# Nine seven-product steps instead of eight, with one weight sum done by an accumulating DMA

## The chip, the cores and the metric

The kernel runs on one core of one Trainium2 chip. The metric is the device time of one execution in microseconds (us). Three executions of the kernel before took 1774.49, 1775.84 and 1777.14 us; their median is 1775.84. The profile is of a further execution.

## The reference: what is computed

The input x has 256 rows of 4096 float32 values. One layer is computed: RMS norm, a projection to q, k, v and a gate (4096 x 16384 weights, `w_in`), stick-breaking attention over 32 heads of 128, the gate, a projection back (4096 x 4096, `w_out`), a residual add and a final RMS norm.

```python
def attn_branch(xn, w_in, w_out):
    proj = xn @ w_in
    q, k, v, g = jnp.split(proj, 4, axis=-1)
    ...                                  # 32 heads: o = stick_breaking_attention(q, k, v)
    return (o * jax.nn.silu(g)) @ w_out

def reference(x, norm_attn, w_in_attn, w_out_attn, ...):
    h = x
    for i in range(DEPTH):               # DEPTH is 1: the attention layer alone
        h = h + attn_branch(rms_norm(h, norm_attn), w_in_attn, w_out_attn)
    return rms_norm(h, final_norm)
```

Nearly all arithmetic is the two projections, over 256 rows and 335 MB of float32 weights.

## The kernel before, in words

**Precision.** A float32 operand is held as two fp32r parts, a high one (`wh`, `nh`) and a remainder (`wl`, `nl`). ScalarE (ACT) rounds a weight block to `wh`, VectorE (DVE) subtracts to get `wl`, and a product of two blocks is three matmuls of 128 x 128 by 128 x 512: wh with h, wl with h, wh with l (`mm3`). The row parts are the stationary operand, the weights the moving one.

**Units, steps, products.** The work is 21 units in a row. Units 0 to 15 are the columns of `w_in`, each with 256 columns of q, k, v and gate; units 16 to 20 are the columns of `w_out`. A unit has 16 steps; a step takes 256 of the 4096 rows of the weights, as two 128-row chunks, for two column groups. So a step is a 2 x 2 block product: row blocks A11, A12, A21, A22 (two halves of the 256 rows of x by two chunks) with weight blocks of two loaded tiles, tile 0 and tile 1, each with chunk 0 and chunk 1. Units 0, 1 and 16 are plain: eight products per step, each added to one of four sums. Units 2 to 15, 17 and 18 are mixed: their steps with a number in `SEVEN` (L42) take seven products of Strassen's kind, and the other steps take eight products arranged so that they add to the same seven sums. Units 19 and 20 are single: four products per step. A seven-step needs sums of weight blocks (`sums`, L386) and sums of row blocks (`build`, L493).

**What a step costs the converters.** An eight-step converts each of its two tiles as one block of 128 x 1024 (`piece`, L410: one cast on ACT, one subtraction on DVE). A seven-step converts tile 0, then one 128 x 512 chunk of tile 1, then makes its sums in place of the tiles by four additions of 128 x 512 on DVE, and converts both tiles again. So it has three conversions of 128 x 1024 and one of 128 x 512.

**Buffers.** Weight tiles land in a ring of seven `raw` tiles of 512 KB (two DMAs of 256 KB from the SP queue each), converted blocks in a ring of five pairs (`PAIRS`) and two singles (`SINGLES`). A tile's buffer is free for the seventh load after its own once it was read for the last time.

**The order of the work** is made at build time by a planner (`Plan`, L89): it plays the program forward with a cost for every piece of work, and each engine takes, of what is ready, the piece with the lowest key (roughly the due time). The order in which the pieces come out is the program order of each engine. On the chip each engine, and each DMA-issuing queue (SP, POOL), works through its own list in that order: whatever stands first and waits holds back all that is behind it. Costs and keys hence move instructions, and cost no time themselves.

**Around the products.** At the end of a mixed unit DVE and ACT combine the seven sums (`combine`, L678); attention for unit u runs during unit u + 1 (`head`, L780), and three POOL DMAs spill its result to DRAM. During units 15 and 16 the spilled parts come back by POOL (`load_parts`, L916: `oh`, `ol`, later `rh`, `rl`; `build_heads`: `p`). In unit 0 the rows of x are loaded once more for the norm (`x_stats`, L595: `xr`).

## Time and profile before

| | |
|---|---|
| median of three runs | 1775.84 us |
| the profiled execution's own time | 1773.91 us |
| its span in the profile | 1772.2 us |
| PE busy | 1752.9 us (99%) |
| PE weight loads busy | 1444.6 us (82%) |
| DVE busy | 1584.7 us (89%) |
| ACT busy | 1117.2 us (63%) |
| POOL busy | 66.9 us (4%) |
| HBM read | 370.43 MB |

PE is the matmul engine, PEld its weight loads, DVE VectorE, ACT ScalarE, POOL GpSimd. The DMA share is the mean busy share of the 16 DMA engines. Matmuls overlap (each shows 0.39 us and the next starts 0.23 us later), so a busy PE alone does not say that it runs at its pace: the count of matmuls in a stretch, or the time from start to start, does. All operations are recorded at line 108, a helper, so groups are told apart by tile names: `acc` is a sum of products, `raw` a loaded weight tile, `wh` and `wl` its parts.

### The profile page before, as it was taken

Reading aid. Unit: us, or ns where it says so; the run is one execution under the profiler, and the core shown is the slowest. Engines: PE = TensorE matmul, PEld = TensorE weight load, DVE = VectorE, ACT = ScalarE, POOL = GpSimd, SP = SyncE. Lnnn points to the kernel's source line nnn. Section 1 sums busy time; section 2 is a strip of 40 time slices with the busy share of each in tenths; the row PEclk is TensorE's granted clock in tenths of the full one; section 3 lists DMA queues with packets and bytes.
Section 4 is the critical chain, followed back from the end, with each engine's and each line's share of the span. In section 5 each row is a group of like instructions: output and inputs, shape, how many; then the busy total and the mean of one; then the engine's idle time right before and its main releaser. Section 6 shows DMA issues by size and latency. Waiting matters only on the chain.

```text
span 1772.2 us, 23794 instructions
## 1 busy us (share of the span) xinstructions
PE 1752.9 (99%) x7883; PEld 1444.6 (82%) x7883; DVE 1584.7 (89%) x2022; ACT 1117.2 (63%) x1520; POOL 66.9 (4%) x132
## 2 busy tenths in 40 slices
PE   8999999999999999999999999999999999999997
PEld 6888888888888888888888888888888888877886
DVE  5688999999999999999999999999999988999963
ACT  6675757575757575767675757575757676555543
POOL 0001000000000000000000000000002200000000
PEclk9999999999999999999999999999999999999999
DMA  9958465657565566665656565656568966668873
GB/s 342 315 184 262 162 213 186 224 178 228 182 216 194 204 201 206 201 204 199 206 202 210 194 215 190 220 187 221 187 212 274 318 227 226 209 219 261 287 253 137
DMA packets 210301, 388.04 MB, mean 219 GB/s; under 512 B 23808, under 2 KB 25088, under 8 KB 210176
## 3 DMA queue, kind: packets, MB, share of 16 engines
q1 hardware_dynamic: 193968, 352.15, 59.7%
q0 software_dynamic: 14624, 31.99, 5.6%
q10 hardware_dynamic: 1584, 2.38, 0.4%
q8 instruction: 62, 1.02, 0.2%
q14 instruction: 63, 0.52, 0.1%
HBM read 370.43 MB, written 15.99 MB: 218 GB/s over the span
## 4 chain that ended last, share of the span: by engine, by line
PE 91%; DVE 4%; ACT 2%; DMA 2%; issue 1%; SPq 0%; ACTq 0%; DVEq 0%
PE acc L108 87%; PE z L108 2%; DVE wl L108 2%; PE o L108 2%; DMA xres<-in_x_dram 1%; DVE raw L108 1%; PE tr L108 1%; ACT wh L108 1%; DMA raw<-in_w_in_dram 1%; DVE h L108 1%; ACT h L108 0%; SPq L108 0%; ACTq L108 0%; ACT f L108 0%; DVE nl L108 0%
## 5 line engine op out<-in xcount | busy, mean ns | idle before, releaser
L108 ACT CAST wh<-raw 128x1024 fp32r<-128x1024 f32 (+1 forms) x898 | 845.1, 986 | 422.8 <-DVE raw L108 204.9
L108 DVE TENSOR_TENSOR wl<-raw,wh 128x1024 fp32r<-128x1024 f32 (+1 forms) x898 | 990.5, 1141 | 125.6 <-ACT wh L108 119.3
L108 PE MATMUL acc<-wh,nh 128*128 128x512 f32 x1680 | 668.8, 398 | 0.0
L108 PE MATMUL acc<-wl,nh 128*128 128x512 f32 x1680 | 656.0, 390 | 0.0
L108 PE MATMUL acc<-wh,nl 128*128 128x512 f32 x1680 | 655.2, 390 | 0.0
L108 PEld LDWEIGHTS acc<-wl,nh 128*128 128x128 f32 x1680 | 315.9, 188 | 66.2 <-DVE wl L108 4.1
L108 PEld LDWEIGHTS acc<-wh,nl 128*128 128x128 f32 x1680 | 315.4, 188 | 65.8
L108 PEld LDWEIGHTS acc<-wh,nh 128*128 128x128 f32 x1680 | 315.7, 188 | 61.9
L108 DVE TENSOR_TENSOR raw<-raw,raw 128x512 f32<-128x512 f32 x384 | 264.7, 689 | 8.8
L108 PE MATMUL acc<-wl,ph 128*128 128x512 f32 x304 | 119.0, 392 | 2.1 <-DVE wl L108 2.1
L108 PE MATMUL acc<-wh,ph 128*128 128x512 f32 x304 | 118.6, 390 | 0.4 <-ACT wh L108 0.2
L108 PE MATMUL acc<-wh,pl 128*128 128x512 f32 x304 | 118.4, 389 | 0.0
L108 PE MATMUL acc<-wh,sh 128*128 128x512 f32 x256 | 102.3, 399 | 1.4 <-DVE sh L108 0.8
L108 PE MATMUL acc<-wh,sl 128*128 128x512 f32 x256 | 101.2, 395 | 2.0 <-DVE sl L108 2.0
L108 PE MATMUL acc<-wl,sh 128*128 128x512 f32 x256 | 100.7, 393 | 0.0
L108 DVE TENSOR_TENSOR raw<-raw 128x512 f32<-128x512 f32 x128 | 88.3, 690 | 3.4
L108 PEld LDWEIGHTS acc<-wl,ph 128*128 128x128 f32 x304 | 57.1, 188 | 15.9 <-DVE wl L108 4.3
L108 PEld LDWEIGHTS acc<-wh,ph 128*128 128x128 f32 x304 | 57.1, 188 | 13.1 <-ACT wh L108 0.6
L108 PEld LDWEIGHTS acc<-wh,pl 128*128 128x128 f32 x304 | 57.1, 188 | 11.6
L108 PEld LDWEIGHTS acc<-wh,sl 128*128 128x128 f32 x256 | 48.8, 190 | 13.0 <-DVE sl L108 2.7
L108 PEld LDWEIGHTS acc<-wh,sh 128*128 128x128 f32 x256 | 48.8, 191 | 12.0 <-issue 1.4
L108 PEld LDWEIGHTS acc<-wl,sh 128*128 128x128 f32 x256 | 48.8, 191 | 9.9
(118 smaller groups left out, 1241.8 us busy)
## 6 DMA issues: line engine op xcount, KB each, us to landing
raw<-in_w_in_dram SPq DMA_DIRECT2D x1020, 256.0 KB, 4.0
raw<-in_w_out_dram SPq DMA_DIRECT2D x256, 256.0 KB, 4.1
xr<-in_x_dram SPq DMA_DIRECT2D x16, 256.0 KB, 5.3
xn<-in_xT_dram POOLq DMA_DIRECT2D x16, 256.0 KB, 4.1
xres<-in_x_dram SPq DMA_DIRECT2D x16, 256.0 KB, 5.0
xs<-in_xT_dram SPq DMA_DIRECT2D x15, 256.0 KB, 5.3
spill_f<-gated POOLq DMA_DIRECT2D x15, 256.0 KB, 2.4
spill_h<-oh POOLq DMA_DIRECT2D x15, 256.0 KB, 2.6
```

Source lines behind the costliest of these rows:

```text
L108: return self.tc.keep_in_program_order(getattr(self.engine, name)(*args, **kw))
```

## The change

It does five things.

1. `SEVEN` gets nine steps per unit instead of eight (1, 3, 5, 7, 8, 10, 11, 13, 14).
2. The sums are a different set (the seven products and the row sums are renamed and re-signed with them, so that `combine` adds at one place where it subtracted): chunk 1 of tile 1 is added to chunk 0 of tile 1, and this is no longer done by DVE but by two DMAs of 128 KB from the POOL queue, which read chunk 1 from DRAM once more and add it to what lies in the tile (`add_block`). DVE keeps three additions. The DMAs wait until the tile has landed; the first DVE addition waits for them.
3. Tile 1 of a seven-step is loaded earlier: ahead of tile 1 of the step before instead of behind tile 0 of its own step.
4. The reloads of row parts start later and one after the other (`later`), and the loads of x for the norm are spread over eleven steps instead of eight.
5. The planner's cost of a POOL DMA goes from 900 to 550 and that of attention's matmuls is changed; keys of the first two pieces of a seven-step are 4000 earlier; two output tiles of the last units take other buffers (one of them a `raw` tile).

```diff
-SEVEN = (1,3,5,7,9,11,13,14)
+SEVEN = (1,3,5,7,8,10,11,13,14)
...
-    (1, BOTH, ((7, "S3", 0), (6, "S2", 1))),
-    (0, BOTH, ((5, "S1", 0), (4, "A22", 1))),
+    (1, BOTH, ((7, "S3", 0), (5, "S1", 1))),
+    (0, BOTH, ((6, "S2", 0), (4, "A22", 1))),
...
-        issue = 900 if engine == "gpsimd" else 330
+        issue = 550 if engine == "gpsimd" else 330
...
+        seven = [parts[quad_parts[q][0]]["seven"] for q in range(len(quads))]
+        tiles = [(2 * q - 1.5 if t and seven[q] else 2 * q + t, q, t) for q in range(len(quads)) for t in range(2)]
+        for _, q, t in sorted(tiles):
...
+            if t and seven[q]:
+                nc.start(add_block(q))
...
+    def add_block(q):
+
+        yield nc.until(("raw", q, 1))
+        w, blocks, s = quads[q][1]
+        r = raw[q, 1]
+
+        def both():
+            for i, c in enumerate(blocks):
+                nc.gpsimd.dma_start(r[:, i, 0, :], w[c, s][:, 1, :], accum_op=ALU.add)
+
+        yield moved("gpsimd", both, [CW] * HG, first[quad_parts[q][0]] - 2e4, after=lambda: nc.tell(("T3", q)), adds=True)
...
-        yield nc.until(("lows", a), ("raw", q, 1))
-        yield add(one, 0, one[:, :, 0, :], two[:, :, 0, :], first[c])
-        yield add(two, 0, two[:, :, 0, :], two[:, :, 1, :], first[c])
+        yield nc.until(("lows", a), ("T3", q))
+        yield add(one, 0, one[:, :, 0, :], two[:, :, 0, :], first[c], ALU.subtract)
         yield nc.until(("lows", b))
-        yield add(two, 1, two[:, :, 1, :], one[:, :, 0, :], first[c])
+        yield add(two, 1, one[:, :, 0, :], two[:, :, 1, :], first[c])
         nc.tell(("sums", c))
-        yield add(one, 1, one[:, :, 1, :], two[:, :, 1, :], first[d])
+        yield add(one, 1, one[:, :, 0, :], one[:, :, 1, :], first[d])
...
-            yield nc.until(("used", 0, i // 2))
+            yield nc.until(("used", 0, 1 + i * 11 // 16))
...
-        yield nc.until(after, ("spilled", s))
+        yield nc.until(*after, ("spilled", s))
...
-        nc.start(load_parts(s, "o", ("used", NB - 1, s)))
+        later = int(8 + 1.3 * s)
+        nc.start(load_parts(s, "o", (("used", NB - 1, s), ("used", NB - 1 + later // NS, later % NS))))
...
-        nc.start(load_parts(s, "r", ("used", LAST - 2, s)))
+        later = int(8 + 1.3 * s)
+        nc.start(load_parts(s, "r", (("used", LAST - 2, s), ("used", LAST - 2 + later // NS, later % NS))))
```

The names below are those of the program with their numbers: `raw136_1` is tile 1 of step 136 of all steps (step 8 of unit 8), the last number counts all tiles. First DVE in unit 8, before: step 137 is a seven-step, with its four additions (the second has one tile name because both its inputs lie in tile 1).

```order
L108 TENSOR_TENSOR wl378_7068<-raw137_0_6944,wh378_7067 128x1024
L108 TENSOR_TENSOR raw137_0_6944<-raw137_0_6944,raw137_1_6959 128x2x256
L108 TENSOR_TENSOR raw137_1_6959<-raw137_1_6959 128x2x256
L108 TENSOR_TENSOR raw137_1_6959<-raw137_1_6959,raw137_0_6944 128x2x256
L108 TENSOR_TENSOR raw137_0_6944<-raw137_0_6944,raw137_1_6959 128x2x256
L108 TENSOR_TENSOR wl380_7084<-raw137_1_6959,wh380_7083 128x1024
L108 TENSOR_TENSOR wl381_7094<-raw137_0_6944,wh381_7093 128x1024
```

DVE at the same place of the program with the change: step 136 is now a seven-step.

```order
L108 TENSOR_TENSOR wl384_7079<-raw135_0_6956,wh384_7078 128x1024
L108 TENSOR_TENSOR a7_1_7084<-a7_1_7084,bound_105 128x256
L108 TENSOR_TENSOR raw135_0_6956<-raw135_0_6956,raw135_1_6931 128x2x256
L108 TENSOR_TENSOR wl389_7095<-raw136_1_6971,wh389_7094 128x512
L108 TENSOR_TENSOR raw135_1_6931<-raw135_0_6956,raw135_1_6931 128x2x256
L108 TENSOR_TENSOR gated7_6966<-o7_1_7100,gated7_6966 128x256
L108 TENSOR_TENSOR raw135_0_6956<-raw135_0_6956 128x2x256
L108 TENSOR_TENSOR wl386_7106<-raw135_1_6931,wh386_7105 128x1024
L108 TENSOR_TENSOR ol7_7124<-gated7_6966,oh7_7123 128x512
L108 TENSOR_TENSOR wl387_7129<-raw135_0_6956,wh387_7128 128x1024
L108 TENSOR_TENSOR wl388_7153<-raw136_0_7030,wh388_7152 128x1024
L108 TENSOR_TENSOR raw136_0_7030<-raw136_0_7030,raw136_1_6971 128x2x256
```

Each step has three additions, and the last row shown, the first addition of step 136, is the one that now waits for the POOL DMAs into `raw136_1`. SP's list with the change, around the load of that tile:

```order
L108 DMA raw133_1_6819<-in_w_in_dram 128x512 x2
L108 DMA raw132_1_6849<-in_w_in_dram 128x512 x2
L108 DMA raw133_0_6869<-in_w_in_dram 128x512 x2
L108 DMA raw134_0_6884<-in_w_in_dram 128x512 x2
L108 DMA raw135_1_6931<-in_w_in_dram 128x512 x2
L108 DMA raw134_1_6945<-in_w_in_dram 128x512 x2
L108 DMA raw135_0_6956<-in_w_in_dram 128x512 x2
L108 DMA raw136_1_6971<-in_w_in_dram 128x512 x2
```

Before, the list was 133_0, 133_1, 134_0, 134_1 and so on; now tile 1 of each seven-step (133, 135, 136) stands ahead of its neighbours, and `raw136_1`, seven loads behind `raw133_1`, takes that tile's buffer. POOL's list with the change, around the end of attention of unit 8:

```order
L108 DMA raw152_1_7778<-in_w_in_dram 128x256 x2
L108 DMA raw154_1_7871<-in_w_in_dram 128x256 x2
L108 DMA spill_f8_7954<-gated8_7773 128x512
L108 DMA spill_h8_7962<-oh8_7930 128x512
L108 DMA spill_l8_7967<-ol8_7931 128x512
L108 DMA raw155_1_7969<-in_w_in_dram 128x256 x2
L108 DMA raw157_1_8043<-in_w_in_dram 128x256 x2
```

Before, POOL held only the three spills of a unit here; now the accumulating DMAs stand around them, and those of step 155 stand behind the spills, which wait for attention's `gated8`, `oh8` and `ol8`.

More of the change, by code (lines that the diff above doesn't have):

```diff
@@ L286 @@
                 )
+    if 0:
+        late, turn = [], []
+        for k, p in enumerate(parts):
+            if p["seven"] and p["i"] > 1 and p["s"] < NS - 1:
+                late.append(p)
+                continue
+            turn.append(p)
+            if late and p["s"] != late[0]["s"] and (p["i"] == 1 if p["seven"] else p["i"] == 0):
+                now = [q for q in late if q["s"] < p["s"] or q["u"] < p["u"]]
+                turn += now
+                late = [q for q in late if q not in now]
+        assert not late and len(turn) == len(parts)
+        parts = turn
     n_parts = len(parts)
@@ L325, in act @@
         return nc.work("scalar", cost, emit, soon() if key is None else key, **kw)
-    FULL_P, FULL_S = (P,) * 4, (S,) * 4
+    FULL_P, FULL_S = (P,) * 2, (W,) * 2
     def ten(emit, *n):
-        return nc.work("tensor", sum(tensor_ns(m) for m in n), emit, nc.here - 1e4, wait=400)
+        return nc.work("tensor", 90 + sum(tensor_ns(m) for m in n), emit, nc.here - 1e4, wait=400)
     def moved(engine, emit, sizes, key, after=None, hold=False, adds=False):
-        issue = 900 if engine == "gpsimd" else 330
+        issue = 550 if engine == "gpsimd" else 330
         return nc.work(
@@ L358, in load, with both @@
     def load():
[L359 to L373 removed]
+        seven = [parts[quad_parts[q][0]]["seven"] for q in range(len(quads))]
+        tiles = [(2 * q - 1.5 if t and seven[q] else 2 * q + t, q, t) for q in range(len(quads)) for t in range(2)]
+        for _, q, t in sorted(tiles):
+            w, blocks, s = quads[q][t]
+            yield nc.take("raw")
+            r = raw[q, t] = wp.tile([P, HG, KT, CW], F32, tag="raw", name=f"raw{q}_{t}", bufs=RAW_BUFS)
+            if t and seven[q]:
+                nc.start(add_block(q))
+            for chunks in [slice(0, 1), slice(1, 2)] if q == 0 else [BOTH]:
+                name = ("raw", q, t, chunks.start) if q == 0 else ("raw", q, t)
+                def both():
+                    for i, c in enumerate(blocks):
+                        nc.sync.dma_start(r[:, i, chunks, :], w[c, s][:, chunks, :])
+                yield moved(
+                    "sync", both, [CW * (chunks.stop - chunks.start)] * HG, first[quad_parts[q][0]] + t,
+                    after=lambda name=name: nc.tell(name),
+                )
+    def add_block(q):
+        yield nc.until(("raw", q, 1))
+        w, blocks, s = quads[q][1]
+        r = raw[q, 1]
+        def both():
+            for i, c in enumerate(blocks):
+                nc.gpsimd.dma_start(r[:, i, 0, :], w[c, s][:, 1, :], accum_op=ALU.add)
+        yield moved("gpsimd", both, [CW] * HG, first[quad_parts[q][0]] - 2e4, after=lambda: nc.tell(("T3", q)), adds=True)
     def tile_done(*tile):
@@ L416, in piece @@
         size = (c.stop - c.start) * W
-        yield act(lambda: nc.scalar.copy(h, full), size, first[n] - 2.0 * 1e3)
-        yield dve(lambda: minus(l, full, h), size, first[n])
+        key = first[n] - (4 * 1e3 if p["seven"] and p["i"] < 2 else 0)
+        yield act(lambda: nc.scalar.copy(h, full), size, key - 2.0 * 1e3)
+        yield dve(lambda: minus(l, full, h), size, key)
         for k in range(c.start, c.stop):
@@ L1041, in mixed_h @@
         if c + 1 == NJ - 3:
-            yield nc.take("s")
+            yield nc.take("s", "s")
         for k in range(2):
@@ L1058, in single_h @@
         yield nc.until(("full", LAST - 1, 1), ("full", LAST - 1, 6), ("used", LAST - 1, NS - 1))
-        yield nc.take("s")
+        yield nc.take("raw")
         new_h(c)
```

48 lines of the change are left out of this document (21 added, 27 removed).

## The prediction

> **What bounds the kernel now.** I read the page's busy shares, then one mixed unit in the stage view, then the chain of waits inside it.
>
> ```profile
> PE 1752.9 (99%) x7883; PEld 1444.6 (82%) x7883; DVE 1584.7 (89%) x2022; ACT 1117.2 (63%) x1520; POOL 66.9 (4%) x132
> ...
> core 0: us, PE busy (x) PEld busy (x) DVE busy (x) ACT busy (x) POOL busy (x), PEclk, DMA share, GB/s
> 700.80:787.96 87.16, 87.16 (x398) 72.06 (x397) 82.50 (x102) 56.48 (x74) 1.61 (x3) 1.00 0.62 202
> ...
> 577.16 0.69 PE o L108 x4
> 577.85 51.71 PE acc L108 x228
> ```
>
> A mixed unit takes 87.16 us, PE is busy for all of it, and the chain of waits there runs through PE alone: 228 matmuls follow each other in 51.71 us, 0.2268 us each, at the granted clock of 1.00. A product (three matmuls) thus costs 0.680 us. The 120 products of a unit are 81.7 us, attention's matmuls the other 5.5. So the mixed stages are bound by the number of matmuls. DVE is next: 82.50 of 87.16 us, 4.7 us to spare per unit. Where DVE falls behind, PE stops, and one stage shows it, in units 17 and 18:
>
> ```profile
> 1500.00:1550.00 50.00, 50.00 (x222) 41.25 (x221) 45.83 (x61) 29.06 (x41) 0.00 (x0) 1.00 0.59 194
> 1550.00:1600.00 50.00, 48.14 (x207) 38.11 (x205) 47.72 (x57) 29.30 (x35) 0.00 (x0) 1.00 0.62 210
> 1600.00:1650.00 50.00, 49.38 (x218) 40.86 (x218) 48.10 (x57) 28.26 (x37) 5.32 (x10) 1.00 0.85 276
> ...
> PEld acc L108 <- DVE wl L108: 4.0, 5, 1.1
> ...
> DVE h L108 <- DMA xres<-in_x_dram: 3.0, 5, 1.3
> ```
>
> A stretch of 50 us holds 50 / 0.2268 = 220.5 matmuls; the second and third hold 207 and 218, so 16 x 0.2268 = 3.6 us are lost there, mostly to DVE's `wl`, and DVE itself waits there for `xres` loads (the last two rows are waits of 1500 to 1640 us: total, times, longest).
>
> **The change part by part.**
>
> *Products.* The rows of PE fall from 7637 to 7589 in the program's order: 48 matmuls, 16 products, one for each of the 16 mixed units. 16 x 0.680 = **10.9 us less**. The Trainium skill (TensorE: Matmul & The Clock Gate, Back-to-back issue gap) gives N / 2.4 + 2.5 ns, 215.7 ns for 512 columns; by that the sum would be 16 x 3 x 0.2157 = 10.4 us. This trace shows 226.8 ns, and the measurement decides.
>
> *DVE and ACT.*
>
> ```profile
> L108 DVE TENSOR_TENSOR wl<-raw,wh 128x1024 fp32r<-128x1024 f32 x766 | 908.2, 1220 | 120.3 <-ACT wh L108 113.9 <-DMA raw<-in_w_in_dram 1.5 <-DMA raw<-in_w_out_dram 0.4
> L108 DVE TENSOR_TENSOR raw<-raw,raw 128x512 f32<-128x512 f32 x384 | 264.7, 689 | 8.8
> L108 DVE TENSOR_TENSOR wl<-raw,wh 128x512 fp32r<-128x512 f32 x132 | 89.1, 684 | 5.3 <-ACT wh L108 5.3
> L108 DVE TENSOR_TENSOR raw<-raw 128x512 f32<-128x512 f32 x128 | 88.3, 690 | 3.4
> ...
> L108 ACT CAST wh<-raw 128x1024 fp32r<-128x1024 f32 x766 | 773.4, 1049 | 366.3 <-DVE raw L108 204.9 <-PE acc L108 106.5 <-issue 30.9
> L108 ACT CAST wh<-raw 128x512 fp32r<-128x512 f32 x132 | 81.6, 618 | 56.5 <-DMA raw<-in_w_in_dram 47.3 <-PE acc L108 4.7 <-DMA raw<-in_w_out_dram 4.2
> ```
>
> Additions per unit: 8 x 4 = 32 before, 9 x 3 = 27 now, five of 0.69 us less. Conversions: one of 128 x 1024 and one of 128 x 512 more. On DVE that is -3.45 + 1.22 + 0.68 = -1.5 us, on ACT 1.05 + 0.62 = +1.7 us. DVE goes to 81.0 us of a unit of 87.16 - 0.68 = 86.5, so its spare time grows from 4.7 to 5.5 us; ACT to 58.2. Neither becomes the bound. In the stage that lost 3.6 us DVE has 3.0 us less over its two units; I take 1 us as won (bounds 0 and 3.0, since the waits for `xres` stay in DVE's list). **1 us less.**
>
> *The accumulating DMAs, what they take.* 16 x 9 x 2 = 288 of 128 KB. No row shows one that adds. On POOL each is one issue; the unit above has three POOL DMAs in 1.61 us, 0.54 each, while DVE is at 95%. 18 x 0.54 = 9.7 us per unit on an engine that is else idle: nothing. On the DMA engines:
>
> ```profile
> q1 hardware_dynamic: 193968, 352.15, 59.7%
> ...
> 1350.00:1400.00 50.00, 50.00 (x226) 41.40 (x226) 47.03 (x56) 29.83 (x37) 12.18 (x23) 1.00 0.94 309
> ```
>
> 352.15 MB are 1343 pieces of 256 KB and take 0.597 x 1772.2 us of all engines: 0.79 us per piece. Adding must fetch the source, fetch the old value and write: at least one plain pass (0.79), at most three (2.4). I take two, 1.6, between the ends. Nine pieces per unit are 7.1 to 21.3 us of 86.5, a share of 0.08 to 0.25 on top of 0.62: 0.70 to 0.87. At a share of 0.94 (second row) PE still lost nothing, so this too is hidden. The cover would be gone where a piece costs over 0.38 x 86.5 / 9 = 3.7 us.
>
> *The accumulating DMAs, when they land.* This is the new wait. DVE works in order: while the first addition waits, every `wl` behind it waits. The tightest step of a unit is step 8 (136): `raw136_1` takes the buffer of `raw133_1`, last read by `wl380`. From there to the addition stand 17 rows of DVE: seven `wl` of 128 x 1024, one of 128 x 512, three additions, and six rows of attention.
>
> ```profile
> 812.05 2.35 DVE L108 TENSOR_TENSOR wl<-raw,wh 128x1024 fp32r<-128x1024 f32 x2
> ...
> L108 DVE SCALAR_TENSOR_TENSOR f<-z,f 128x384 f32<-128x384 f32 x32 | 17.8, 557 | 20.3 <-ACT f L108 20.3
> L108 DVE TENSOR_TENSOR fl<-f,fh 128x384 fp32r<-128x384 f32 x32 | 17.6, 551 | 0.0
> L108 DVE TENSOR_TENSOR f<-f,bound 128x256 f32<-128x256 f32 x32 | 13.6, 424 | 1.0
> L108 DVE TENSOR_TENSOR a<-a,bound 128x256 f32<-128x256 f32 x32 | 13.4, 418 | 1.0 <-ACT a L108 1.0
> L108 DVE TENSOR_TENSOR gated<-o,gated 128x256 f32<-128x256 f32 x32 | 13.3, 416 | 0.4 <-ACT gated L108 0.4
> L108 DVE TENSOR_TENSOR ol<-gated,oh 128x512 fp32r<-128x512 f32 x16 | 10.9, 684 | 0.0
> ...
> raw<-in_w_in_dram SPq DMA_DIRECT2D x1020, 256.0 KB, 4.0
> xn<-in_xT_dram POOLq DMA_DIRECT2D x16, 256.0 KB, 4.1
> spill_l<-ol POOLq DMA_DIRECT2D x15, 256.0 KB, 2.3
> rl<-spill_l POOLq DMA_DIRECT2D x8, 256.0 KB, 5.6
> raw<-in_w_in_dram SPq DMA_DIRECT2D x8, 128.0 KB, 3.3
> ...
> DMA to landing us min/median/max: 2.2/4.0/9.4
> ```
>
> Two `wl` take 2.35 us, not 2.44, so an instruction starts some 0.08 before the one ahead ends: 7 x 1.22 + 0.68 + 3 x 0.69 + 3.05 (the six) less 17 x 0.08 is 13.0 us. Counted alike, the other eight steps have 15.4 (11 and 14), 16.6 (13) and 18.9 to 24.4. Needed: the tile's load 4.0 and its second issue 0.4, two POOL issues 1.1, and the landing of the second accumulating DMA. Its ends are a plain POOL transfer at its quickest, 2.3, and three passes of a load by POOL one after the other, 3 x 4.1 = 12.3; I take 5, among the loads by POOL of 4.1 to 5.6, which are the nearest rows. That is 10.5 of 13.0: the addition finds its data, and what is late next is nothing. **0 us**; the margin is 13.0 - 5.5 = 7.5 us of landing time. By the Trainium skill (DMA: Bandwidth & Descriptors, Anatomy of one DMA) one lands after about 2.0 us + bytes / 436e3, 2.3 us for 128 KB; the 3.3 us of the 128 KB row is above it, and no run so far shows an adding one. With 2.3 us the margin would be wider and the slower rival below rarer.
>
> POOL's list is in order as well: in each unit step 155's kind stands behind the three spills. Its addition has 15.4 us from its buffer's last reader, and `ol` stands before that reader on DVE, so the spills are issued before the tile has landed.
>
> *Tile 1 earlier, reloads and `xr` spread, buffers, keys.* Same DMAs, other times. The reloads that made the 0.94 above cost PE nothing there, so spreading them wins nothing; the latest now starts four steps ahead of its use, 4 x 4 x 0.68 = 10.9 us in the single units, against 5.6 to land. In the first 100 us PE stops once after its start, and has the load share of 0.97 beside it:
>
> ```profile
> 0.00:50.00 50.00, 45.30 (x177) 34.61 (x178) 29.64 (x40) 30.05 (x47) 1.57 (x10) 0.93 0.97 346
> ...
> 28.13 0.50 PE L108 MATMUL acc<-wh,sh 128*128 128x512 f32 x1 [0.60 <-ACT sh L108]
> ...
> 1700.00:1750.00 50.00, 50.00 (x223) 41.40 (x222) 27.57 (x29) 21.72 (x26) 0.00 (x0) 1.00 0.55 178
> ```
>
> At most 0.6 us is to be had; I take 0. The output tile in a `raw` buffer takes one of seven places in the last unit, where the share is 0.55 and PE full (last row): 0.
>
> **Sum.** -10.9 - 1 = -11.9 us. The profiled execution took 1773.91 us (span 1772.2 and 1.7 around it): 1762.0. The median of the runs is 1.9 above that execution, so **1764 us**, a ratio of 0.9933.
>
> **The rivals.**
>
> *More comes back.* All 3.0 us of DVE's relief in units 17 and 18 and the 0.6 at the start are won: 1764 - 2.6 = 1761. For it: PE waits for `wl` there. Against it: DVE stays at 94% in the mixed units. I keep it in the forecast's own range, 1759 to 1769.
>
> *Part of it is lost to late landings.* A wait of DVE stops PE only when the converted blocks run out. These are at most five pairs ahead; a seven-step uses three pairs for six products, so five pairs are 10 x 0.68 = 6.8 us, and half of it where the ring is not full. A landing of 11 us makes step 8 wait 11 - 7.5 = 3.5 us, so from there up some of the 0.68 us per unit goes: 1769 to 1779. For it: single loads of `raw` took up to 9.4 us (last row of that fence), and steps 10, 11 and 13, 14 stand side by side. Against it: 4.1 us for 256 KB by the same queue.
>
> *Slower: DVE becomes the bound by waiting.* One mechanism, at the first addition of a seven-step. With a landing time L step 8 waits L - 7.5. That wait lies inside the 15.4 us of step 11, which then has enough; step 13 waits L - 11.1, step 14 the rest to L - 9.9. So a unit waits 2L - 17.4. DVE's 5.5 us of spare time and the 11.9 / 16 = 0.7 us won are used up at 2L - 17.4 = 6.2, L = 11.8 us, some three times the plain load. At the upper end, 12.3, it is 7.2 us, 1.7 more than DVE has: 16 x 1.7 = 27 us lost against 11.9 won, 1776 + 15 = **1791 us**, and each further us of landing costs 32. For it: no row shows an adding DMA, and the price is steep past the point. Against it: every plain row by POOL is at half of it or less.
>
> *That the change does not do what it says* is excluded by the 48 rows of PE.
>
> **How the numbers follow.** Forecast with its own range 1759 to 1769: 0.77. Part lost, 1769 to 1779: 0.12. Slower: 0.11. No change can be told from a measurement of this kernel within about 0.2%, 3.6 us, so 1772.3 to 1779.4 is "same". Of the 0.12 some 0.05 lies below 1772.3: faster 0.82, same 0.07, slower 0.11. The range reaches from the most that comes back into the partly lost case: 1759 to 1773, 0.82 of the chance.
>
> **What would show it right or wrong.** Right: PE 48 matmuls fewer; a mixed unit of 86.5 us with PE busy throughout; DVE near 81 us per unit; POOL some 155 us busier (288 x 0.54); a DMA share of 0.70 to 0.87 in the mixed units; few or no waits of DVE `raw` for the DMA into `raw`; fewer lost matmuls around 1550 to 1650 us. Wrong: a median landing of the accumulating DMAs above 7.5 us, waits of `wl` for such a DMA, units longer than 87.16 us, or the mixed units as forecast and the gain lost in the reload stages.

## The result: 1762.0 us, and the profile after

The changed kernel took 1762.0 us, median of four runs (1759.72 to 1763.35), against 1775.16 us before (median of four, 1773.76 to 1777.14). The ratio is 0.9924, with a 95% interval of 0.9907 to 0.9941. Forecast were 1764 and 0.9933. The profiled execution is the longest of the four: 1763.35 us, span 1761.4.

From the page of the kernel after: busy time by engine, two DMA queues (packets, MB, share of 16 engines), and the issues of weight tiles (count, size, median us to landing).

```profile
PE 1743.5 (99%) x7835; PEld 1434.6 (81%) x7835; DVE 1547.2 (88%) x1982; ACT 1142.3 (65%) x1554; POOL 320.9 (18%) x422
...
q1 hardware_dynamic: 193968, 352.15, 60.5%
q0 software_dynamic: 56384, 70.28, 20.2%
...
raw<-in_w_in_dram SPq DMA_DIRECT2D x1020, 256.0 KB, 4.6
...
raw<-in_w_in_dram POOLq DMA_DIRECT2D x252, 128.0 KB, 5.1
```

The accumulating DMAs are the 252 (and 36 more on `w_out`) of POOL. They land after 5.1 us. The share of POOL's queue q0 rose from 5.6% to 20.2%: 0.146 x 1761.4 = 257 us of all 16 engines for 144 sums of 256 KB, 1.8 us each, where a plain 256 KB takes 0.79.

Four units of the kernel after in the stage view (stretch, length, busy time of PE, weight loads, DVE, ACT, POOL with counts, granted clock, DMA share, GB/s): a mixed unit, unit 15 with the first reloads, and units 17 and 18.

```profile
537.76:624.49 86.73, 86.69 (x396) 71.51 (x395) 80.07 (x98) 57.91 (x76) 17.36 (x21) 1.00 0.81 232
1318.54:1405.37 86.83, 86.79 (x396) 71.58 (x395) 79.95 (x97) 58.51 (x76) 24.23 (x36) 1.00 0.91 270
1497.28:1579.89 82.61, 81.86 (x358) 66.78 (x357) 76.72 (x90) 52.87 (x67) 15.66 (x18) 1.00 0.83 242
1579.89:1662.65 82.76, 81.91 (x358) 66.69 (x357) 77.97 (x92) 48.55 (x59) 21.88 (x32) 1.00 0.93 275
```

The same mixed unit and units 17 and 18 of the kernel before, cut at its own bounds:

```profile
541.57:628.72 87.15, 87.15 (x398) 72.06 (x396) 82.53 (x101) 56.59 (x74) 1.61 (x3) 1.00 0.59 203
...
1505.84:1589.62 83.78, 82.59 (x361) 67.36 (x360) 78.06 (x92) 49.05 (x63) 0.00 (x0) 1.00 0.63 208
1589.62:1673.56 83.94, 82.66 (x361) 67.29 (x360) 80.86 (x96) 48.16 (x59) 8.48 (x16) 1.00 0.82 264
```

A mixed unit fell from 87.15 to 86.73 us, 0.42 and not the 0.68 of the product it no longer has. POOL went from 1.61 to 17.36 us, and DVE does not wait for it there: in the whole execution DVE waits for an accumulating DMA once, for 0.4 us, in units 17 and 18.

**The ledger.** Every product matmul is in the traces, so a unit can be cut at the start of its first one. The table gives us per unit, in the profiled executions; the plain and single units hold as many products before as after. Units 0 to 3 differ by up to 2 us between kernels that are alike up to there.

| units | before | after | change | forecast |
|---|---|---|---|---|
| start, 0, 1 (plain) | 192.2 | 191.0 | -1.2 | 0 |
| 2, 3 | 175.0 | 173.3 | -1.7 | -1.4 |
| 4 to 14 | 958.9 | 954.2 | -4.7 | -7.5 |
| 15 (first reloads) | 87.2 | 86.8 | -0.4 | -0.7 |
| 16 (plain) | 92.55 | 91.9 | -0.6 | 0 |
| 17, 18 | 167.7 | 165.4 | -2.4 | -2.4 |
| 19, 20 | 87.0 | 87.0 | 0 | 0 |
| sum | | | -10.9 | -11.9 |

So the sum came out, but the units that were to bring most of it brought 6.8 of 9.5 us, and the start and the units without a product fewer brought 1.8 us, of which 0.7 are in unit 0, within that spread. The ledger is of two profiled executions, the longest of four after and one of the shorter before; the medians differ by 13.2 us, and where the 2.3 us beyond the ledger lie isn't known.

**Where 0.26 us per unit went.** Here are the waits of the weight loads in nine mixed units (engine, line, what it waited for; total, times, longest), first of the kernel before, then of the kernel after.

```profile
PEld acc L108 <- DVE wl L108: 2.8, 9, 0.3
PEld o L108 <- ACT gated L108: 1.8, 9, 0.2
```

```profile
PEld o L108 <- DVE a L108: 4.1, 9, 0.5
PEld z L108 <- DVE fl L108: 2.4, 9, 0.4
PEld o L108 <- ACT gated L108: 1.8, 9, 0.2
```

Before, products waited a little for `wl` in every unit. Now they do not, but attention's matmuls (`o`, `z`) wait for DVE's `a` and `fl`. Some of such a wait hides behind the matmul before, so I also summed the time from each matmul's start to the next, less 0.2268 us for a product matmul, over these nine units. Between products that fell from 12.3 to 10.3 us, around attention it rose from 37.4 to 41.7. Per unit: -0.68 (the product) - 0.22 (waits for `wl`) + 0.48 (attention) = -0.42.

### The profile page after: what moved, and what is told of

It is laid out like the page before. It is cut to its first block, busy times and chain, and to the rows that moved or that the text cites. A ratio compares the mean times of both kernels' runs of the same rounds, so it can differ in the third digit from the quotient of the medians.

```text
span 1761.4 us, 24831 instructions
## 1 busy us (share of the span) xinstructions
PE 1743.5 (99%) x7835; PEld 1434.6 (81%) x7835; DVE 1547.2 (88%) x1982; ACT 1142.3 (65%) x1554; POOL 320.9 (18%) x422
## 3 DMA queue, kind: packets, MB, share of 16 engines
q0 software_dynamic: 56384, 70.28, 20.2%
## 4 chain that ended last, share of the span: by engine, by line
PE 81%; DVE 3%; DMA 2%; issue 1%; ACT 1%; SPq 0%; ACTq 0%; DVEq 0%
PE acc L108 77%; PE z L108 2%; DVE wl L108 2%; PE o L108 2%; DMA xres<-in_x_dram 1%; PE tr L108 1%; DMA raw<-in_w_out_dram 1%; DVE raw L108 0%; SPq L108 0%; ACT h L108 0%; ACT wh L108 0%; DVE h L108 0%; ACTq L108 0%; DVE pl L108 0%; ACT sq L108 0%
## 5 line engine op out<-in xcount | busy, mean ns | idle before, releaser
L108 ACT CAST wh<-raw 128x1024 fp32r<-128x1024 f32 (+1 forms) x930 | 874.6, 980 | 470.8 <-issue 188.0
L108 DVE TENSOR_TENSOR wl<-raw,wh 128x1024 fp32r<-128x1024 f32 (+1 forms) x930 | 1020.3, 1136 | 149.9 <-ACT wh L108 142.2
L108 PE MATMUL acc<-wl,nh 128*128 128x512 f32 x1666 | 649.4, 390 | 0.0
L108 POOL DMA_DIRECT2D raw<-in_w_in_dram x252 | 220.3, 985 | 949.8 <-DMA raw<-in_w_in_dram 416.3
L108 DVE TENSOR_TENSOR raw<-raw,raw 128x512 f32<-128x512 f32 x288 | 197.9, 687 | 4.3 <-DMA raw<-in_w_out_dram 0.4
L108 PE MATMUL acc<-wh,ph 128*128 128x512 f32 x294 | 114.6, 390 | 0.0
L108 PE MATMUL acc<-wh,pl 128*128 128x512 f32 x294 | 114.6, 390 | 0.0
L108 DVE TENSOR_TENSOR raw<-raw 128x512 f32<-128x512 f32 x144 | 98.5, 684 | 0.0
L108 PEld LDWEIGHTS acc<-wl,ph 128*128 128x128 f32 x294 | 55.2, 188 | 15.7 <-DVE wl L108 4.3
L108 PEld LDWEIGHTS acc<-wh,pl 128*128 128x128 f32 x294 | 55.2, 188 | 11.1
L108 PEld LDWEIGHTS acc<-wh,sl 128*128 128x128 f32 x256 | 48.5, 189 | 13.2 <-DVE sl L108 3.1
```

The lines of the kernel that those rows point to most:

```text
L108: return self.tc.keep_in_program_order(getattr(self.engine, name)(*args, **kw))
```

## The experiments

My theory was the sum of the prediction: the gain is 16 products and DVE's relief in units 17 and 18; the early tile 1 gives more spare time than is needed; the spread loads win nothing. Twelve kernels were run; all compute the whole layer. Each ratio is to runs of the kernel before on the same chip (medians 1774.5 to 1775.1).

### Nine steps without the accumulating DMA (e1_nine_dve)

The kernel before, with:

```diff
-SEVEN = (1,3,5,7,9,11,13,14)
+SEVEN = (1,3,5,7,8,10,11,13,14)
```

> The kernel before with nine seven-steps in the places of the change, all four additions still on DVE, nothing else changed. Theory (products set the time only as long as DVE keeps below the unit; the accumulating DMA is what makes room for the ninth step): PE has 48 matmuls fewer, a pure 86.5 us per mixed unit, but DVE gets 1.22 + 0.68 + 4 x 0.69 = 4.7 us more per unit, 82.5 + 4.7 = 87.2 us, above the unit itself. DVE becomes the bound: units of 87.5 to 88.5 us, 1777 to 1792 us in all. Rival (the count of products alone decides): 1775 - 10.9 = 1764 us, the same as the change.

Measured: 1793.28 us, ratio 1.0105 (1.0092 to 1.0118). A mixed unit in the stage view, and PE's waits in nine of them:

```profile
543.09:631.29 88.20, 87.13 (x394) 71.33 (x393) 85.78 (x107) 57.75 (x76) 1.61 (x3) 1.00 0.59 200
```

```profile
PE acc L108 <- DVE wl L108: 9.6, 18, 0.6
```

With four additions per step DVE has 85.78 of 88.20 us, PE stops for `wl` (9.6 us in nine units, 1.07 each), and a unit is 1.05 us longer than before in spite of three matmuls fewer. Units 17 and 18 are 6.7 us longer together, and the time lies 1.3 us above the expected range. In this order of the work the ninth step costs time unless DVE is relieved; the theory holds here.

### The accumulating DMA with eight steps (e2_eight_acc)

The kernel after, with:

```diff
-SEVEN = (1,3,5,7,8,10,11,13,14)
+SEVEN = (1,3,5,7,9,11,13,14)
```

> The change with the old eight seven-steps: accumulating DMAs, early tile, spread loads and all the rest, but the old count of products. Theory (nearly the whole gain is the 16 products): 10.9 us above the change, 1771 to 1775 us, DVE near 77 us of an 87.2 us unit, units at 87.2 us. Rival (the accumulating DMA or the spread loads win time by themselves): 1766 us or less.

Measured: 1766.47 us, ratio 0.9953 (0.9940 to 0.9965), 0.5 us above what the rival said and far below the theory's 1771. Without one product fewer, some 8 of the 13 us are there; the ninth step adds 4.5, and every run of this kernel lies above every run of the kernel after. So it is wrong to credit nearly the whole gain to the products. A mixed unit and units 17 and 18 of this kernel:

```profile
539.87:626.89 87.02, 87.02 (x397) 72.14 (x396) 77.27 (x93) 57.02 (x75) 15.56 (x19) 1.00 0.79 227
...
1502.58:1584.70 82.12, 81.94 (x361) 67.49 (x360) 73.64 (x86) 49.97 (x64) 13.31 (x16) 1.00 0.83 238
1584.70:1666.80 82.10, 81.88 (x361) 67.49 (x360) 75.50 (x88) 48.00 (x58) 19.70 (x29) 1.00 0.95 284
```

The ledger of this kernel against the one before: up to unit 3 -1.4 us (within the spread named above), units 4 to 15 -1.2, unit 16 -0.6, units 17 and 18 -3.5, in all -6.8 in the profiled executions. Units 17 and 18 have DVE 4.4 and 5.4 us lighter, and are shorter than in the kernel with nine steps (82.61 and 82.76), although they have three matmuls more each. The waits of the weight loads for `wl` in these two units, before, in this kernel, and in the kernel after (total, times, longest):

```profile
PEld acc L108 <- DVE wl L108: 4.3, 6, 1.1
...
PEld acc L108 <- DVE wl L108: 0.6, 1, 0.6
...
PEld acc L108 <- DVE wl L108: 4.3, 7, 1.1
```

With DVE 9.8 us lighter over the two units the waits for `wl` are nearly gone, and in the kernel after they are as before, so there the ninth step costs 1.1 us more than it brings. That this is DVE's load alone is not shown: with nine steps and the planner's old cost of attention's matmuls (e7_ten_cost below) DVE has 77.00 and 78.33 us in these units, about as in the kernel after, the wait is 0.6 us again, and the two take 162.4 us together, less than the 164.2 here. The order counts as much as the load.

### No spreading of reloads and loads (e3_no_spread)

The kernel after, with:

```diff
-        later = int(8 + 1.3 * s)
+        later = s
...
-            yield nc.until(("used", 0, 1 + i * 11 // 16))
+            yield nc.until(("used", 0, i // 2))
...
-        yield nc.until(("form", "s", 0))
+        yield nc.until(("used", 0, 0))
```

> The change with the loads of x over eight steps again, reloads of row parts as early as before and the constant after the first step as before. Theory (these are worth little: the start of the profiled execution was 2 us better, partly by a shorter stretch at half clock): 1762 to 1765 us. Rival (the spread reloads keep the DMA engines free for the accumulating DMAs near 1350 to 1450 us, where the share is 0.9 to 1.0 already): PE loses matmuls there, 1768 us or more.

Measured: 1772.46 us, ratio 0.9989 (0.9980 to 0.9998): 10.5 us slower than the kernel after. The prediction had this part at 0, and the rival's time holds. Units 0 to 14 together take the same as in the kernel after (unit 15 begins at 1318.69 and 1318.54 us); all of the loss is in the two units into which reloads fall, 15 and 18:

```profile
1318.69:1409.46 90.77, 88.28 (x392) 72.11 (x390) 80.68 (x98) 58.51 (x75) 32.05 (x50) 0.98 1.00 297
...
1584.11:1674.24 90.13, 84.46 (x358) 68.75 (x357) 79.74 (x94) 49.07 (x59) 22.23 (x32) 0.96 0.93 278
```

They lose 3.9 and 7.4 us. The x loads and a constant that the change prepares earlier in unit 0 thus are worth nothing, the reloads all of it. The granted clock shows a second price, in this stretch of unit 18:

```profile
1626.00:1630.30 4.30, 1.61 (x6) 0.76 (x5) 4.30 (x7) 3.38 (x5) 2.02 (x3) 1.00 1.00 288
1630.30:1637.10 6.80, 5.61 (x13) 4.45 (x14) 6.80 (x10) 2.98 (x6) 0.67 (x2) 0.50 1.03 331
1637.10:1640.50 3.40, 3.40 (x16) 2.75 (x16) 2.58 (x3) 1.99 (x3) 2.25 (x3) 0.99 0.88 209
```

PE is busy for 1.6 of 4.3 us, and in the 6.8 us after that the clock is 0.50: 13 matmuls, where 16 fit into half that time afterwards. Behind the stop the same stage costs a second time. POOL's waits in these units, first unit 15, then unit 18:

```profile
POOL oh L108 <- PE acc L108: 47.9, 13, 7.3
...
POOL rh L108 <- PE acc L108: 43.0, 8, 9.1
```

A reload stands in POOL's list and waits until PE has read the old row part, and the accumulating DMAs stand behind it. In the kernel before such waits are there too (111.2 us in unit 15), and nothing that anyone waits for stands behind them. Whether these waits are what costs, the next two runs ask.

### Reloads two and eight steps later (e9_two_later, e12_eight_later)

The kernel after, with this for both kinds of reloads (in e12_eight_later `s + 8`):

```diff
-        later = int(8 + 1.3 * s)
+        later = s + 2
```

> The changed kernel, with each reload of a row part issued two steps after the step that frees its buffer, instead of from eight steps after on and spread over 1.3 times as many steps. So the reloads come as densely as without the spreading (one pair per step), only some 10 us later. The run without any spreading lost 10.5 us, all in two units: 3.9 in the one that carries the first reloads, 7.4 in the one that carries the second. Theory, POOL's order: there a reload stands in POOL's list and waits for PE to read the old contents (40.7 and 43.0 us of such waits in the two units), and the accumulating DMAs stand behind it. Two steps later PE has read them, the waits are gone, and the time is that of the changed kernel, 1762 to 1764. Rival, bandwidth: the DMA engines are too full when reloads and accumulating DMAs fall together (share 0.98 to 1.03); then the loss stays, 1769 to 1773. Between the two both have a part.

> The changed kernel, with each reload eight steps after the step that frees its buffer, one per step: the delay of the changed kernel without its factor 1.3. Two steps later gave 1770.4 against 1762.0, with 91.2 us in the first unit with reloads (86.8 in the changed kernel, 90.8 with no delay) and 84.3 in the second (82.8 and 90.1). Theory: what counts is into which unit the reloads fall; eight steps later half of them come in the next unit, which has no accumulating DMAs. Then the two units take 87 and 83 us and the time is 1762 to 1764. Rival: the density counts, one pair per step is too many beside accumulating DMAs; then the first unit keeps some 2 us or more of its loss and the time is 1766 or above.

Measured: two steps later 1770.42 us (ratio 0.9972, 0.9963 to 0.9981), the time of the rival; eight steps later 1763.77 (0.9937, 0.9925 to 0.9950), that of the theory. Units 15 and 18 with two steps, with POOL's waits for PE in unit 15 between them; then the two units with eight steps.

```profile
1319.84:1411.08 91.24, 88.77 (x397) 72.50 (x395) 80.95 (x99) 58.52 (x75) 31.77 (x50) 0.98 0.99 299
...
POOL oh L108 <- PE acc L108: 15.9, 4, 4.7
...
1584.72:1668.99 84.27, 82.09 (x358) 66.80 (x357) 80.30 (x95) 49.77 (x60) 22.64 (x33) 1.00 1.00 305
```

```profile
1319.06:1405.90 86.84, 86.81 (x396) 71.57 (x395) 80.18 (x98) 58.41 (x76) 26.34 (x40) 1.00 0.92 272
...
1580.56:1661.68 81.12, 81.12 (x358) 66.93 (x357) 78.38 (x93) 48.70 (x59) 21.90 (x32) 1.00 0.94 283
```

Eight steps later, one reload pair per step, is as good as spread by 1.3: the density is not the cause, and the factor 1.3 is not needed. Nor is a full DMA system as such: here are the stretch without spreading in which PE stops, and the end of unit 15 with eight steps, at the same DMA share and more GB/s, where PE is full.

```profile
1375.00:1385.00 10.00, 7.61 (x33) 5.73 (x31) 6.70 (x9) 4.82 (x6) 5.77 (x8) 0.98 1.16 346
...
1390.00:1405.90 15.90, 15.90 (x73) 13.15 (x72) 15.20 (x18) 9.89 (x12) 4.80 (x9) 1.00 1.15 389
```

With eight steps half of the first reloads fall out of the mixed unit; whether that or the longer delay is what helps, no run separates. Two steps later, unit 18 has most of its loss back and unit 15 nothing, though POOL's waits there fell from 47.9 to 15.9 us. So POOL's waiting at run time isn't the cause in unit 15. There the order of DVE differs. Its list in unit 15 without spreading, and with eight steps:

```profile
1372.13 3.50 DVE L108 TENSOR_TENSOR wl<-raw,wh 128x1024 fp32r<-128x1024 f32 x3 [0.64 <-ACT wh L108]
1378.04 0.69 DVE L108 TENSOR_TENSOR wl<-raw,wh 128x512 fp32r<-128x512 f32 x1 [2.41 <-ACT wh L108]
...
1380.13 0.69 DVE L108 TENSOR_TENSOR raw<-raw,raw 128x512 f32<-128x512 f32 x1
```

```profile
1372.51 3.50 DVE L108 TENSOR_TENSOR wl<-raw,wh 128x1024 fp32r<-128x1024 f32 x3 [0.64 <-ACT wh L108]
1376.04 1.42 DVE L108 TENSOR_TENSOR raw<-raw,raw 128x512 f32<-128x512 f32 x2
```

After the same three `wl`, one kernel makes its additions at once, and the other stands idle for 2.41 us and makes them 4 us later. The planner, which plays POOL's list forward too, had placed them there. PE stops at 1382 us, for 1.7 and 0.8 us, and the clock falls to 0.5 for 3.4 us. The data of those additions were there. The two accumulating DMAs of that step were issued in the stretch from 1366 to 1368 us, and land after (last number, median):

```profile
raw<-in_w_in_dram POOLq DMA_DIRECT2D x2, 128.0 KB, 7.8
```

The second one landed at 1375.03 us, before DVE fell idle at 1375.63, and the first addition came at 1380.13. In all of units 15 and 18 without spreading the first addition of a step comes 2.5 us or more after the landing, and DVE has no wait for an accumulating DMA in either. So on the chip these DMAs were in time, and what costs, in unit 15, is the place that the planner gave the additions. For unit 18 the lists were not compared, and no run had the order of the one with the DMAs of the other.

### The reloads spread in the kernel before (e10_before_spread)

The kernel before, with this for both kinds of reloads:

```diff
-        nc.start(load_parts(s, "o", ("used", NB - 1, s)))
+        later = int(8 + 1.3 * s)
+        nc.start(load_parts(s, "o", (("used", NB - 1, s), ("used", NB - 1 + later // NS, later % NS))))
```

> The kernel before, with only the reloads spread as in the changed kernel: no accumulating DMA, eight steps of seven products, its own orders of additions. Theory: without accumulating DMAs nothing stands behind a reload in POOL's list that anyone waits for soon, so spreading is worth nothing there: 1774 to 1776, the units with reloads at 87.2 and 83.9 us as before. Rival: reloads in a crowd cost the kernel before too, through the DMA engines' share of 0.94; then it gets 1770 or less.

Measured: 1775.17 us, ratio 1.0000 (0.9991 to 1.0009). In the sum it is worth nothing there, as the theory has it, but not because nothing moves: unit 15 takes 90.4 instead of 87.2 us and unit 17 takes 82.2 instead of 83.8, with no relief of DVE at all. A part that is worth 10.5 us in one kernel is worth 0 in the other, so an effect of the parts together is shown.

### Tile 1 in its plain place (e4_tile_late)

The kernel after, with:

```diff
-        tiles = [(2 * q - 1.5 if t and seven[q] else 2 * q + t, q, t) for q in range(len(quads)) for t in range(2)]
+        tiles = [(2 * q + t, q, t) for q in range(len(quads)) for t in range(2)]
```

> The change with tile 1 of a seven-step loaded in its plain place, behind tile 0 of its own step: one and a half places later, 1.5 x 2.7 = 4.1 us. In the profile after, the needed time of a seven-step's first addition is 4.6 + 0.4 (load) + 2 x 0.88 (POOL) + 5.1 (landing) = 11.9 us. Theory (the early tile is what hides the landing): without it the additions wait some 3 us at step 8 and 1 us or less at others, and the waits are near DVE's 6.6 us of spare time per unit: 1763 to 1772 us, with waits of DVE for the DMA into raw in every unit. Rival (the landing is hidden with a wide margin): 1762 us and no such waits. Other rival (every seven-step stalls): 1790 us or more.

Measured: 1786.58 us, ratio 1.0064 (1.0051 to 1.0077): 24.6 us slower than the kernel after, between all that was expected. Units 4 to 14 take 970.6 us instead of 954.2, 1.5 each, and units 15 and 18 lose 5.3 and 3.5. From the issue of the second accumulating DMA to the first addition there are 7.9 us in the median (12.8 in the kernel after), by pairing the two in the order of time. DVE itself waits for an accumulating DMA only 8.0 us in nine units; ACT shows more, in nine mixed units without and then with the early tile:

```profile
ACT wh L108 <- DVE raw L108: 158.9, 65, 3.6
```

```profile
ACT wh L108 <- DVE raw L108: 50.0, 36, 2.8
```

The planner counts the later landing in and moves the additions back, and the casts of the sums wait for them; that this is the way the time is lost fits the two rows, and no run isolates it. The early tile is not mere spare time, it is part of the price of the accumulating DMA.

### Later landings (e5_delay_a, e6_delay_b)

The kernel after, with 18 memsets of a scratch tile between the two accumulating DMAs of a step (36 in e6_delay_b):

```diff
             for i, c in enumerate(blocks):
+                for _ in range(18 * i):
+                    nc.gpsimd.memset(pause, 0.0)
                 nc.gpsimd.dma_start(r[:, i, 0, :], w[c, s][:, 1, :], accum_op=ALU.add)
```

> The changed kernel, with 18 small memsets (128x128, of a scratch tile nobody reads) on POOL between the two accumulating DMAs of each step of seven products: nothing but a delay of the second one, about 18 x 0.2 = 3.6 us as an estimate. The trace of the changed kernel has 4.6 (load of the tile) + 0.4 + 2 x 0.88 (issue) + 5.1 (landing) = 11.9 us from the free buffer to the landed half tile against 13.0 us at the tightest step. Theory: the tightest step of a unit then waits 2.5 us, DVE has 86.7 - 80.1 = 6.6 us to spare per unit, so most of it is hidden: 1762 to 1767. Rival: any wait of DVE goes through to PE, 2.5 us for each of 16 units or more: 1800 and up.

> The changed kernel with 36 of those memsets in each step of seven products, 36 x 0.205 = 7.4 us between the two accumulating DMAs. With 18 of them (3.7 us) no mixed unit in the middle became longer. In the changed kernel DVE comes to the first addition 10.8 to 15 us after the second accumulating DMA was issued, of which its landing needs 5.1; with 18 memsets 6.1 to 10.8. Theory: with 36 that falls to 2 to 7 us, so DVE waits 2 to 3 us at steps 11, 13 and 14 and hardly elsewhere; DVE has 6.6 us to spare per unit, and the wait shows as rows of DVE for the DMA into raw, but a unit grows by less than 1.5 us: 1767 to 1785. Rival, by the sum of the prediction: 5.5 + 5.1 + 7.4 + 0.7 is 18.7 of 13.0 us, a wait of 5.7 at step 8 and some 10 us in a unit, more than DVE has: 1800 and up.

Measured: with 18 memsets 1765.66 us (ratio 0.9950, 0.9936 to 0.9964), with 36 of them 2144.76 us (1.2080, 1.2061 to 1.2098). The delays are longer than the two expectations say. They count some 0.2 us for a memset, the length of its row, but the next one starts 0.26 to 0.28 us after the start of the one before. One step's memsets on POOL, first 18, then 36:

```profile
547.22 5.01 POOL L108 MEMSET pause<- 128x128 f32 x18
...
643.88 10.04 POOL L108 MEMSET pause<- 128x128 f32 x36
```

From the issue of the first DMA of a step to that of the second there are 0.6 us in the median of the kernel after, 5.8 with 18 memsets and 10.6 with 36: the delays are 5.2 and 10.0 us. A mixed unit with each, DVE's waits in that of the second, and the engines' shares of the chain that ended last in the second:

```profile
537.95:624.68 86.73, 86.70 (x396) 71.47 (x395) 80.11 (x98) 57.89 (x76) 51.25 (x187) 1.00 0.80 233
```

```profile
634.37:745.99 111.62, 95.83 (x396) 75.62 (x395) 80.40 (x98) 58.13 (x76) 85.33 (x353) 0.92 0.66 184
...
DVE raw L108 <- DMA raw<-in_w_in_dram: 22.2, 6, 5.1
...
POOL 39%; issue 18%; DVE 11%; PE 8%; DMA 8%; ACT 6%; SPq 0%; POOLq 0%; ACTq 0%; DVEq 0%
```

The first delay vanishes in the middle units: units 4 to 14 take 954.2 us, as without it, and what is lost is lost in units 2, 3, 15 and 18 (4.2 us in the profiled execution; unit 17 wins 1.5). There are 10.8 to 15.3 us from the second issue to the first addition in a unit of the kernel after, and 6.6 to 10.2 with this delay, still over the landing. The wait of 2.5 us that the expectation had at the tightest step isn't there, so its time came out for another reason than it gave.

With the second delay DVE waits 22.2 us in a unit. My expectation for it (hidden up to 1.5 us per unit) fails, and the rival's time holds, in more than its size. But this run is no clean test of a late landing. In the unit shown POOL waits for 7.6 of 111.6 us, so its own list, nine delays of 10 us and the DMAs, takes 104 us (102 on average over units 4 to 14), where a whole unit of the kernel after takes 86.7. POOL itself had become the bound, and it leads the chain that ended last. An addition that is late also reads its tile late, so the buffer comes free late and the next tile is loaded late, and a step can hand its wait on; and the clock is 0.92 in the unit. What each of these adds to POOL's list no run shows. So a delay of 5.2 us is hidden, and where between 5.2 and 10.0 us the margin ends stays open.

### The planner's old cost of attention's matmuls (e7_ten_cost, e13_wait)

The kernel after, with:

```diff
-    FULL_P, FULL_S = (P,) * 2, (W,) * 2
+    FULL_P, FULL_S = (P,) * 4, (S,) * 4
...
-        return nc.work("tensor", 90 + sum(tensor_ns(m) for m in n), emit, nc.here - 1e4, wait=400)
+        return nc.work("tensor", sum(tensor_ns(m) for m in n), emit, nc.here - 1e4, wait=400)
```

In e13_wait `wait` is 1000 as well.

> The changed kernel with one thing undone: the planner's cost of attention's small matmuls is that of the kernel before again (no 90 ns extra, four sizes instead of two), so those matmuls and the work that feeds them get other places in the order. In the trace of the changed kernel nine mixed units hold 0.9 us more in the matmuls that write o and 0.9 us more in those that write z from fl than the kernel before, 0.2 us per unit, and a unit takes 86.72 us where 16 x 0.680 less in all would give 86.49. Theory: the new cost puts attention's inputs (a, fl) later than PE reaches them. Then the waits of PE for a and fl go, a unit takes 86.5 us, and the time is 13 x 0.2 = 2.6 us shorter, 1759.5 us. Rival: the waits come from DVE's fuller order with nine steps of seven products; then a unit stays at 86.7 and the time at 1762.

> The kernel with the planner's old cost of attention's matmuls (1760.4), and the planner's distance from an input of attention to the matmul that reads it raised from 400 to 1000 ns, so that such a matmul stands later in PE's order. The sums of idle time between matmuls over nine mixed units say why the ninth step won 0.42 us per unit instead of 0.68: beside the products, attention's matmuls lose 4.3 us in nine units (1.6 before o, 1.0 inside o, 0.6 and 0.9 inside z, 0.2 inside tr), 0.48 per unit, while the products themselves lose 2.0 us less, 0.22 per unit. With the old cost 2.7 of the 4.3 us stay. Theory: these are matmuls that reach their place before a, fl and fh are there; 0.6 us later the inputs are there, the units fall from 86.56 to 86.3 us and the time to some 1757. Rival: the inputs are late by more, or the whole chain moves back with them; then a unit stays at 86.5 or above, and the time at 1760 or above.

Measured: old cost 1760.36 us (0.9924, 0.9911 to 0.9938), between theory and rival, and by the ratio it can't be told from the kernel after; with the longer distance 1767.00 (0.9953, 0.9940 to 0.9967), the rival's side. Waits of the weight loads in nine mixed units, with the old cost, then with the longer distance:

```profile
PEld o L108 <- ACT gated L108: 4.3, 18, 0.3
PEld z L108 <- DVE fl L108: 2.4, 9, 0.3
```

```profile
PEld o L108 <- ACT gated L108: 8.0, 9, 0.9
```

| nine mixed units, us | before | eight steps, acc. | after | old cost | longer distance |
|---|---|---|---|---|---|
| between products | 12.3 | 10.4 | 10.3 | 10.3 | 11.1 |
| around attention | 37.4 | 38.2 | 41.7 | 40.1 | 43.8 |
| a unit | 87.17 | 87.04 | 86.75 | 86.57 | 87.07 |

The old cost takes the wait for `a` away and leaves that for `fl`: 86.57 instead of 86.75 us. The longer distance takes both away and brings a longer one, for `gated`. So attention's place in PE's order does cost 0.1 to 0.7 us per unit, as the theory had it, and the theory fails in that moving all its matmuls by one number doesn't remove it. Each order of this planner has its own loss there. That the changed cost takes 0.18 us per unit with nine steps is shown; with eight steps and the same cost attention loses only 0.09 in all, so the ninth step brings the rest of the 0.48, and why it does is not shown.

### Ten steps (e11_ten_steps)

The kernel of e7_ten_cost, with:

```diff
-SEVEN = (1,3,5,7,8,10,11,13,14)
-SEVEN_OUT = SEVEN
+SEVEN = (1,2,4,5,7,8,10,11,13,14)
+SEVEN_OUT = (1,3,5,7,8,10,11,13,14)
```

> The changed kernel with the planner's old cost of attention's matmuls (which alone gave 1760.4) and ten steps of seven products in each of the 14 mixed units of the first half (1,2,4,5,7,8,10,11,13,14), nine in the two others. 14 products less are 9.5 us. From eight steps to nine DVE's work grew by (720.9 - 695.6) / 9 = 2.8 us per unit, so ten are 82.9 us of DVE in units of 85.9. Theory: DVE at 96.5% is as full as with nine steps and all additions on it (97.2%, where PE lost 1.1 us per unit), so a unit loses 0.4 to 1 us for the 0.68 won: 1757 to 1765, no clear gain. Rival: the spare time of 3.0 us per unit is enough, PE stays full: 1751 to 1754.

Measured: 1774.34 us, ratio 0.9993 (0.9984 to 1.0002). A mixed unit and unit 15, and PE's waits in nine units:

```profile
541.24:628.25 87.01, 86.19 (x394) 71.03 (x392) 83.14 (x103) 59.53 (x78) 19.18 (x23) 1.00 0.81 232
1325.73:1420.09 94.36, 89.65 (x394) 72.96 (x392) 85.09 (x105) 60.82 (x78) 25.88 (x38) 0.96 0.90 274
```

```profile
PE acc L108 <- DVE wl L108: 7.7, 18, 0.5
```

DVE at 83.14 of 87.01 us (95.6%) makes PE wait for `wl` again; a unit is 0.5 us longer than with nine steps instead of 0.68 shorter. The theory's mechanism holds and its price was too small: unit 15 alone loses 7.7 us more. Of eight, nine and ten steps nine is the fastest with this planner, and no version tried beats the changed kernel by more than the measurement can tell.

## Why the prediction was right, point by point

**The time.** 1762.0 against 1764, within the forecast's own range. The profiled execution went from 1773.91 to 1763.35, where the sum had 1762.0. The sum is right partly because two errors cancel, as the ledger shows; that they are of one size is luck. Its split is wrong: with eight steps the rest of the change brings 8.3 us, where the sum has 1 beside the products.

**Products, -10.9 us.** The 48 matmuls are gone (7296 of `acc` to 7248), and 0.2268 us each holds: one run of products in a unit went from 228 matmuls in 51.71 us to this piece of the chain of waits (start, length):

```profile
573.24 51.06 PE acc L108 x225
```

The failed step is "81.7 us, attention's matmuls the other 5.5": I took attention's share as fixed. It grew by 0.48 us per unit, and in units 17 and 18 the ninth step lost more than it brought. So the ninth step is worth 4.5 us and not 10.9 (eight steps against nine).

**DVE and ACT.** DVE fell by 2.5 us per mixed unit, forecast 1.5 (the lengths of its rows fell by 1.6, and the rest is that more of them overlap); ACT rose by 1.3, forecast 1.7. That DVE is not the bound is right for nine steps with the accumulating DMA, and the runs on both sides (nine steps on DVE alone, ten with it) show how little room there is. What I missed: DVE did cost the mixed units something before (waits of `wl`, 0.3 us per unit), so its relief won 0.22 us there too.

**Units 17 and 18, -1 beside the products.** Together -2.4, as in the sum, though the weight loads still wait 4.3 us for `wl` (PE's own waits for it fell from 2.1 to 1.5), and DVE's waits for `xres`, which I took as fixed, rose from 3.0 to 5.3. In the other kernels with nine steps and the accumulating DMA (but for the long delay) the same products and additions take 162 to 172 us there, so to hit 165.4 is in part luck.

**What the accumulating DMAs take.** 1.8 us of all engines per 256 KB against my 1.6, DMA share 0.81 in the forecast 0.70 to 0.87. POOL's busy time is 0.88 us per DMA instead of 0.54, so POOL rose by 254 us instead of 155; nothing hung on it.

**When they land, 0 us.** 5.1 us against the 5 assumed; the Trainium skill (DMA: Bandwidth & Descriptors, Anatomy of one DMA) gives 2.3 us as an estimate for 128 KB, and the accumulating ones are above it by more than twice. That nobody waits is right but for the 0.4 us above. The count of rows that gave 13.0 us at step 8 was too strict: DVE's list has gaps, and the trace has 13.3 us there from the issue alone, with the tightest steps at 11, 13 and 14.

**The slower rival.** Its mechanism, an addition that waits for its DMA, is seen with the late tile 1 and with the long delay. Its point, a landing of 11.8 us, lies between 9.6 us (4.4 + 5.2, nothing lost in the mixed units 4 to 14) and 15.7 (5.7 + 10.0, lost). Its price, "each further us of landing costs 32", wasn't tested: at 15.7 us it gives some 136 us of loss and 383 were measured, but there POOL's own list alone is longer than a unit.

**Tile 1 earlier, reloads and `xr` spread: 0.** This step failed. "The reloads that made the 0.94 above cost PE nothing there, so spreading them wins nothing" read the trace of a kernel without accumulating DMAs. With them unspread reloads cost 10.5 us. A late tile 1 costs 24.6; the count of the landing already had the early one in it, so there the term is right for the change as it is and says nothing of what the part is worth. As the change has both, the sum did not feel it; had it lacked one, the forecast would have been 10 to 25 us too low. For `xr` and the constant the 0 is right.

**The rivals "more comes back" and "part of it is lost"** both happened, in different places: 1.8 us more in the plain units and the start (0.7 of it in the spread of unit 0), 2.7 us lost in the input units, but not by late landings.

## What to carry to other kernels

When a change moves work to a queue that is worked through in order, look again at everything else in that queue: reloads whose crowding cost nothing before cost 10.5 us beside the accumulating DMAs. Where a planner makes the order, compare the lists before blaming the chip: here the data had landed, and the additions stood too late. Split a measured gain by stage before crediting it to the term that was largest on paper; here the eight-step variant had some 8 of 13 us without a product fewer. Spare time can hide a late arrival completely, so test a margin by a delay instead of multiplying out a price, measure how long the delay really is, and count whether the engine that makes it still has the time for it.

## What the runs showed of the hardware

An accumulating DMA of 128 KB from DRAM keeps POOL busy for 0.88 us in the profile, where the plain ones of the kernel before show 0.54. Plain ones beside them grow too (0.94 us in the mean of 15 spills), and the second of a pair starts 0.6 us after the first, so this is not the pace of issue. It lands after 4.2 to 6.5 us in the medians of these runs, and takes the DMA engines some 2.3 times the time of plain bytes (1.8 against 0.79 us per 256 KB).

In the kernel without spreading a stop of PE by 2.5 us (1.7 and 0.8, in unit 15) is followed by 3.4 us at a granted clock of 0.50, and one of 3.9 us (1.6 and 2.3, in unit 18) by 6.8 us, so half of that time comes on top of the stop. Not every stop has this: one of 1.8 us at 1649 us in the same run is followed by full clock. The Trainium skill (TensorE: Matmul & The Clock Gate, What's actually happening) has a window of 3.4 us in which the clock is decided; the two stretches are one and two of these. The kernel with the long delay has 50 stretches at 0.50, and a clock of 0.90 to 0.95 in units 6, 15, 17 and 18.
